# An output projection by seven half-size products, with weight sums made earlier on VectorE

## The chip, the cores and the metric

The kernel runs on one core of a Trainium2 chip. The metric is the time of one execution in device microseconds. Each core has five engines that run their own instruction streams side by side: TensorE (PE, matrix products; its weight loads are listed apart as PEld), VectorE (DVE), ScalarE (ACT), GpSimd (POOL) and SyncE (SP, which issues most transfers). They wait for each other by semaphores. Matrix products are summed in PSUM, which the kernel uses as eight banks of 128 x 512 fp32; all other tiles lie in SBUF, 128 partitions wide.

## The reference

One layer of a decoder with two token mixers, for 1024 tokens and a width of 1024:

```python
h = rmsnorm(x, norm_g)
proj = h @ w_in                                  # split into the parts below
o_gla = gla_chunked(g_q, g_k, g_v, log_a)        # gated linear attention, 4 heads
y_a = (rmsnorm(o_gla, gla_norm_g) * silu(g_gate)) @ w_pa
y_b = (stick_breaking(s_q, s_k, s_v) * silu(s_gate)) @ w_pb     # 8 heads
gates = sigmoid(m_logits + b_gate)
merged = gates[0] * y_a + gates[1] * y_b
out = rmsnorm(x + merged @ w_o, final_g)
```

The change is about the last line: `merged` and `w_o` are both 1024 x 1024. All is fp32 in and out.

## The kernel before, in words

**Products in two halves.** Each fp32 operand of a large product is split into a high part in the matmul's own fp32 format and a low part, the rest: ScalarE writes `hi` (a copy that rounds), VectorE writes `lo = src - hi` (`split`, lines 158 and 159). A product is then three matmuls: hi x hi, hi x lo and lo x hi. Operands that are used as a 1024 x 1024 matrix lie in four quarters (`quarter`): 512 tokens (half n) by the even or the odd blocks of 128 of the inner dimension (parity), each as a pair of tiles of 4 x 512 columns.

**Seven products.** Most parts of `w_in` (28 blocks of 256 columns, `pair_job`) already go by Winograd's form of Strassen's method: with sums of quarters of the activations (S1 to S4, made once) and sums of the quarters of the weight block (`tt`: T1 to T4, four GpSimd instructions per block, lines 233 to 236), seven half-size products (`unit` 0 to 6) replace eight. `Pairs.run(n)` issues the next n of the 28 x 7 units, with the loads and splits of the next blocks between them. A unit is 12 matmuls of 512 columns into one of three PSUM banks (`pp`); VectorE (line 296) or ScalarE (line 265) evicts, and a later unit of the same block adds into the same bank after that.

**The stages.** (1) Norm of x, transposes, the first value columns. (2) The remaining value columns, with S1 to S4. (3) Units of the pairs; over the first 22 of them the GLA decays are computed (`djobs`, pool `dq`), then come 27 units with nothing beside them, `pairs.run(49 - len(djobs))`. (4) The GLA recurrence (from line 683), four units between two steps. Its small factors `fac` (lines 689 to 693) are VectorE instructions, its q, k and v are loaded by SP (lines 701, 702, 711). (5) Stick-breaking attention, filled with `w_pa` products. (6) The `w_pb` products with the merge (`m_half`): 8 column blocks of 128 by 2 token halves, each 24 matmuls; the result is scaled by the gate, the other branch is added, and both halves of the split are written to the four quarters `mq` that stay in SBUF. (7) The output projection.

**The output projection before** (lines 1048 to 1093) works by blocks of 128 tokens: the block's slice of `mq` is the stationary operand, `w_o` the moving one. Columns 0 to 255 come first for all eight token blocks (`proj_n` with `wsA`), while the other 768 columns of `w_o` are loaded and split into `wB`; then for each token block 512 and 256 columns. That is 8 x 24 x 3 = 576 matmuls, 192 of 512 and 384 of 256 columns. `finish` adds x to the bank on VectorE, squares on ScalarE with a running sum, and multiplies by `final_g`; after the last part, `r` is made (VectorE, then a power on GpSimd), VectorE scales columns 0 to 639 and ScalarE the rest, and SP and ACT store them.

**What sets the order.** Instructions are written in program order and a scheduler reorders those of each engine at build time; inside `manual_schedule` the named engines keep the written order. At run time each engine works strictly in its order; a waiting instruction holds all behind it. Buffers of a pool rotate: a tile's next user waits until the last one is done.

Of the kernel before, what the change touches and what calls it, by code (L numbers as in the profile page):

```python
# [9 lines left out]
F32 = mybir.dt.float32  # L10
F32R = mybir.dt.float32r
# [4 lines left out]
P = 128  # L16
# [83 lines left out]
def hybrid_layer(ctx: ExitStack, tc: tile.TileContext, x, norm_g, w_in, w_up, b_dec,  # L100
# [32 lines left out]
    d_a21 = dram_set("a21", 2, [P, 4, HALF])  # L133

# [528 lines left out]
    pairs.run(49 - len(djobs))  # L663
    dq_ctx.close()

# [336 lines left out]
    pq = ctx.enter_context(tc.tile_pool(name="pq", bufs=1, reuse_waits="tile"))  # L1002
    pb_ctx = ExitStack()
# [5 lines left out]
    mq = {}  # L1009
# [22 lines left out]
    mq.update(quads_in(a21b, "m"))  # L1032

    def m_half(pt, eb, n):
        o = stage().bitcast(F32)
        merge_gate(o[:, 0], d_gb, 8, eb, n)
        nc.sync.dma_start(o[:, 1], d_ma[eb][:, half(n)])
        nc.vector.tensor_mul(o[:, 0], pt, o[:, 0])
# [5 lines left out]
    for eb in range(KB):  # L1044
        line += ([pb_load(eb + 2)] if eb + 2 < KB else []) + [pb_unit(eb, 0), pb_unit(eb, 1)]
    Line(line).run()

    wsA = rows_of(load_w256(w_o, 0))
    fg = pq.tile([P, D], F32, tag="fg", name="fg", bufs=1)
    nc.sync.dma_start(fg, final_g.partition_broadcast(P))  # L1050
    xA = pq.tile([P, NT, DV], F32, tag="xA", name="xA", bufs=1)
    nc.sync.dma_start(xA, x2[:, 0:DV].rearrange("(b p) c -> p b c", p=P))
    ssq = pq.tile([P, NT, 3], F32, tag="ssq", name="ssq", bufs=1)
    pb_ctx.close()
    po = ctx.enter_context(tc.tile_pool(name="po", bufs=2, side="right", reuse_waits="tile"))
    wB = [[po.tile([P, D - DV], F32R, tag=f"wo{s}{k}", name=f"wo{s}{k}", bufs=1) for k in range(KB)]
          for s in "hl"]
    ygA = po.tile([P, NT, DV], F32, tag="ygA", name="ygA", bufs=1)
    for kb in range(KB):
        raw = raw_tile().rearrange("p a b -> p (a b)")[:, 0:D - DV]  # L1060
        nc.sync.dma_start(raw, w_o[kb * P:(kb + 1) * P, DV:D])
        split(raw, wB[0][kb], wB[1][kb])
# [54 lines left out]
```

## Time and profile before

| | |
|---|---|
| timed runs, median of 3 | 1256.83 us (1254.66 to 1257.61) |
| the profiled execution | 1258.84 us, its span 1256.8 us |
| PE busy | 1229.9 us, 98% of the span |
| VectorE, ScalarE, GpSimd busy | 768.6, 538.5, 275.0 us |
| mean granted clock of TensorE | 0.995 |
| moved by DMA | 212.08 MB, 169 GB/s |
| output projection | from 1159.89 us, last matmul starts 1250.31 |

Times in rows are microseconds from the span's start. A row of the timeline gives start, duration, engine, line, operation, `out<-in`; in brackets the idle time ahead of it and what ended it. A row of groups gives the same with the count, then busy time and mean ns of one, then idle time ahead. A row of windows gives the window and its length, then busy time and count of PE, PEld, DVE, ACT and POOL, the granted clock, the DMA share and GB/s. A row of DMA issues ends in KB of each and the median us from issue to landing. Matmuls are pipelined: one of 512 columns is shown as 0.39 us long, while the next starts about 0.23 us after it.

### The profile page before, as it was taken

The page shows a single profiled execution, that of the slowest core. Times are in us where ns is not written, and L with a number is a line of the kernel's source. Part 1 is how long each engine was busy: PE and PEld are TensorE (multiplying, and loading weights), DVE is VectorE, ACT ScalarE, POOL GpSimd, SP SyncE. Part 2 cuts the span into 40 slices and gives each one's busy share as a digit, 9 for nine tenths or more (in the row PEclk, how much of TensorE's full clock was granted, in tenths as well). Part 3 has the DMA queues.
Part 4 walks back from the last instruction along what each step waited for, and adds up shares of the span by engine and source line. Part 5 has one row for each costly group of instructions (what it writes and reads, how often), then busy time and mean ns, then how long its engine had stood idle before and what let it go on. Part 6 is the DMA issues. An engine that isn't in the chain of part 4 may idle for free. (4 is left out here: it accounts for less than half of the span.)

```text
span 1256.8 us, 18168 instructions
## 1 busy us (share of the span) xinstructions
PE 1229.9 (98%) x6579; PEld 1034.1 (82%) x6579; DVE 768.6 (61%) x1313; ACT 538.5 (43%) x1042; POOL 275.0 (22%) x296
## 2 busy tenths in 40 slices
PE   8999999999999999999999999999889999999998
PEld 8999878888888888888888878778777878888986
DVE  5474874456655676666654367778867775354533
ACT  5344663344344444444433244445554554233322
POOL 2495331322242242332323010000100000000010
PEclk9999999999999999999999999999989999999999
DMA  7553456555564555755535755444675438553232
GB/s 270 185 172 107 151 190 189 166 155 175 166 199 140 165 187 172 227 172 193 183 124 169 248 160 157 161 155 152 206 222 167 139 105 275 175 167 112 83 117 93
DMA packets 191574, 212.08 MB, mean 169 GB/s; under 512 B 11478, under 2 KB 145644, under 8 KB 188924
## 3 DMA queue, kind: packets, MB, share of 16 engines
q1 hardware_dynamic: 190332, 209.34, 51.4%
q10 hardware_dynamic: 1152, 1.57, 0.3%
q8 instruction: 52, 0.85, 0.3%
q14 instruction: 38, 0.31, 0.1%
HBM read 133.28 MB, written 77.59 MB: 168 GB/s over the span
## 5 line engine op out<-in xcount | busy, mean ns | idle before, releaser
L159 DVE TENSOR_TENSOR wl<-tt,wh 128x1024 fp32r<-128x1024 f32 x56 | 69.0, 1232 | 73.1 <-ACT wh L158 72.8
L296 DVE TENSOR_TENSOR f<-pp,f 128x512 f32<-128x512 f32 x84 | 57.9, 689 | 91.0 <-PE pp L261 87.2
L158 ACT ACTIVATE wh<-raw 128x1024 fp32r<-128x1024 f32 x57 | 60.2, 1058 | 95.9 <-PE pp L260 48.8
L159 DVE TENSOR_TENSOR wl<-raw,wh 128x1024 fp32r<-128x1024 f32 x57 | 80.0, 1405 | 33.3 <-ACT wh L158 32.4
L158 ACT ACTIVATE wh<-tt 128x1024 fp32r<-128x1024 f32 x56 | 59.3, 1059 | 83.0 <-PE pp L260 82.4
L875 POOL TENSOR_SCALAR_AFFINE_SELECT be<-be 128x128 f32<-128x128 f32 x64 | 22.9, 359 | 282.1 <-ACT be L867 214.6
L265 ACT ACTIVATE f<-pp 128x512 f32<-128x512 f32 x84 | 49.6, 591 | 73.0 <-PE pp L261 67.9
L233 POOL TENSOR_TENSOR tt<-raw 128x512 f32<-128x512 f32 x28 | 38.5, 1375 | 184.6 <-DVE wl L159 153.0
L873 DVE TENSOR_TENSOR_SCAN eb<-eb 128x128 f32<-128x128 f32 (+6 forms) x56 | 71.8, 1282 | 5.6 <-ACT eb L866 3.1
L220 POOL TENSOR_TENSOR r<-r,nhalf 128x1 f32<-128x1 f32 x40 | 23.7, 593 | 207.9 <-DVE r L219 207.9
L866 ACT ACTIVATE eb<-z 128x384 f32<-128x384 f32 (+4 forms) x96 | 48.4, 505 | 42.1 <-PE z L864 28.7
L158 ACT ACTIVATE ath<-tr 128x512 fp32r<-128x512 f32 (+2 forms) x96 | 44.0, 496 | 37.9 <-PE tr L892 37.0
L159 DVE TENSOR_TENSOR atl<-tr,ath 128x512 fp32r<-128x512 f32 (+2 forms) x96 | 51.1, 545 | 6.3 <-ACT ath L158 6.3
L909 PE MATMUL av<-atl,v 128*128 128x256 f32 x160 | 47.2, 295 | 3.9 <-DVE atl L159 3.9
L892 PE MATMUL tr<-ident,be 128*128 128x128 f32 x288 | 44.8, 279 | 5.1 <-DVE be L878 4.2
L197 PE MATMUL pp<-bh,wh 128*128 128x512 f32 x128 | 49.8, 389 | 0.0
L198 PE MATMUL pp<-bl,wh 128*128 128x512 f32 x128 | 49.8, 389 | 0.0
L199 PE MATMUL pp<-bh,wl 128*128 128x512 f32 x128 | 49.8, 389 | 0.0
L878 DVE TENSOR_TENSOR be<-be,eb 128x128 f32<-128x128 f32 (+3 forms) x64 | 48.3, 754 | 2.4 <-DVE eb L873 0.5
L892 PEld LDWEIGHTS tr<-ident,be 128*128 128x128 f32 x288 | 32.9, 141 | 19.9 <-DVE be L878 9.9
L867 ACT ACTIVATE be<-z 128x384 f32<-128x384 f32 (+4 forms) x96 | 49.0, 512 | 0.0
L550 ACT ACTIVATE o<-o,vcol 128x512 f32<-128x512 f32 x32 | 23.1, 723 | 59.0 <-DMA o<-d_gb 35.4
(411 smaller groups left out, 4045.8 us busy)
## 6 DMA issues: line engine op xcount, KB each, us to landing
raw<-in_w_in_dram SPq DMA_DIRECT2D x31, 1024.0 KB, 6.0
d_v<-o SPq DMA_DIRECT2D x32, 256.0 KB, 3.0
d_gv<-o SPq DMA_DIRECT2D x32, 256.0 KB, 3.8
v<-d_gv SPq DMA_DIRECT2D x32, 256.0 KB, 3.3
d_q<-o SPq DMA_DIRECT2D x16, 512.0 KB, 4.3
d_k<-o SPq DMA_DIRECT2D x16, 512.0 KB, 5.2
k<-d_k SPq DMA_DIRECT2D x8, 1024.0 KB, 5.1
v<-d_v SPq DMA_DIRECT2D x8, 1024.0 KB, 7.2
```

The lines of the kernel that those rows point to most:

```text
L158: nc.scalar.activation(hi, src, AF.Copy)
L159: eng.tensor_sub(lo, src, hi.bitcast(F32))
L197: nc.tensor.matmul(pt, whi[:, kb], h_, start=kb == 0, stop=False)
L198: nc.tensor.matmul(pt, whi[:, kb], l_, start=False, stop=False)
L199: nc.tensor.matmul(pt, wlo[:, kb], h_, start=False, stop=kb == KB - 1)
L265: nc.scalar.activation(t[nm], t[bank], AF.Copy)
L296: nc.vector.tensor_add(add, bank, add)
L866: nc.scalar.activation(om[:, osl], zt[:, 0:w], AF.Sigmoid, scale=-inv_sqrt)
L867: nc.scalar.activation(be[:, osl], zt[:, 0:w], AF.Sigmoid, scale=inv_sqrt)
L873: nc.vector.tensor_tensor_scan(rest, rest, rest, om[:, T - P:T - P + 1], op0=ALU.mult, op1=ALU.min)
L878: nc.vector.tensor_mul(be[:, off:T], be[:, off:T], om[:, off + 1:T + 1])
L892: nc.tensor.transpose(pt[:, b * P:(b + 1) * P], be[:, c:c + P], ident)
```

## The change

The output projection, too, goes by the seven products, over both token halves and both column halves of `w_o` at once.

- **Sums of w_o.** T1 to T4 of `w_o` (four sums of 128 x 512 for each of four row pairs) are made by VectorE among the 27 units after the decays, and stored to DRAM (`d_t`). SP loads and stores around them. These units now run one at a time with these jobs between them; the pool `dq` is closed ahead of them.
- **Sums of merged.** In stage 6 only the first token half is split at once (A11, A12). GpSimd makes S1 to S4 from the four pieces of each block pair, SP stores S1 to S4 and A22 to DRAM (`d_s`). The last two blocks run in the order (6,0), (7,0), (6,1), (7,1). B11 and B21 of `w_o` are loaded and split between the units, and T1, T2 and most of S2 are loaded.
- **The products.** 28 items of 12 matmuls of 512 columns: seven products by four blocks of 128 tokens, in seven PSUM banks (four `xb`, three `pp`). x is loaded in whole rows. VectorE adds each bank to its x block right after the item (for the first five somewhat later), ScalarE squares when a half row is complete, VectorE applies `r` and `final_g` in one instruction. The other operands are loaded and split item by item (`parts`, `loads`). PE, ACT and DVE keep the written order.

VectorE in the 27 units after the decays, before, from the copies of the decays' last columns (`ebl`) on; `f<-pp,f` is an eviction, `wl`, `dl` and `o` are low halves:

```order
L647 COPY ebl<-e 128x16
L159 TENSOR_TENSOR wl<-tt,wh 128x1024
L689 MEMSET fac 128x48 x2
L690 TENSOR_TENSOR fac<-ebl 128x8
L692 COPY fac<-ebl 128x8
L693 COPY fac<-ebl 128x8
L691 COPY fac<-fac 128x8
L690 TENSOR_TENSOR fac<-ebl 128x8
L692 COPY fac<-ebl 128x8
L693 COPY fac<-ebl 128x8
L296 TENSOR_TENSOR f<-pp,f 128x512
```

The same engine there with the change (`t<-t` is a sum of `w_o`):

```order
L299 TENSOR_TENSOR f<-pp,f 128x512
L162 TENSOR_TENSOR wl<-raw,wh 128x1024
L162 TENSOR_TENSOR o<-tr,o 128x512
L681 TENSOR_TENSOR t<-t 128x512 x3
L162 TENSOR_TENSOR wl<-tt,wh 128x1024
L681 TENSOR_TENSOR t<-t 128x512
L299 TENSOR_TENSOR f<-pp,f 128x512
L681 TENSOR_TENSOR t<-t 128x512 x3
L299 TENSOR_TENSOR f<-pp,f 128x512
```

The `fac` block has gone from here to two weight blocks later (behind the last sums), and three sums in a row stand ahead of evictions.

VectorE in the output projection before, for one token block:

```order
L1067 TENSOR_TENSOR y<-pp,y 128x512
L1070 TENSOR_TENSOR yg<-y,fg 128x512
L1085 TENSOR_SCALAR pre<-ssq 128x1
L1067 TENSOR_TENSOR y<-pp,y 128x256
L1070 TENSOR_TENSOR yg<-y,fg 128x256
L1087 TENSOR_SCALAR r<-ssq,pre 128x1
L1090 TENSOR_SCALAR yg<-yg,r 128x640
```

With the change, from the add of item 14 (a first-half block, product S4 x B22) to that of item 17, the last row, which is the first use of the last x block:

```order
L1209 TENSOR_TENSOR ya<-pp,ya 128x512
L1146 TENSOR_TENSOR mS3l<-raw,mS3h 128x1024
L1225 TENSOR_SCALAR pre<-ssq,pre 128x1
L1209 TENSOR_TENSOR y<-pp,y 128x512
L1234 SCALAR_TENSOR_TENSOR ya<-ya,pre,fg 128x1024
L1146 TENSOR_TENSOR mS3l<-raw,mS3h 128x1024
L1209 TENSOR_TENSOR ya<-pp,ya 128x512
L1146 TENSOR_TENSOR wT4l<-tt,wT4h 128x1024
L1225 TENSOR_SCALAR pre<-ssq,pre 128x1
L1209 TENSOR_TENSOR ya<-pp,ya 128x512
```

Adds now alternate with low halves of operands that later items need. SP's last rows with the change:

```order
L1126 DMA raw<-d_sA_182 128x1024
L1126 DMA raw<-d_sA_183 128x1024
L1230 DMA out_dram<-ya 128x1024
L1184 DMA ya<-in_x_dram 128x1024
L1230 DMA out_dram<-ya 128x1024 x3
L1230 DMA out_dram<-y 128x512 x3
L1230 DMA out_dram<-ya 128x512
```

The one x load among the stores is that last block's (`ya` has four buffers, and it is the fifth tile).

The diff, cut to its core:

```diff
     manual.close()
-    pairs.run(49 - len(djobs))
     dq_ctx.close()
...
+    def t_load(j):
+        wt[j] = tq.tile([P, 4, HALF], F32, tag="t", name="t")
+        for two in range(2):
+            nc.sync.dma_start(wt[j][:, 2 * two:2 * two + 2], ...)
+    def t_sum(j, i):
+        dst, x1, x2_ = ((0, 1, 0), (1, 3, 1), (3, 3, 0), (2, 2, 3))[i]
+        nc.vector.tensor_sub(wt[j][:, dst], wt[j][:, x1], wt[j][:, x2_])
+    def t_store(j):
+        nc.sync.dma_start(d_t[j][:], wt[j])
+    tjobs = [[] for _ in range(49 - len(djobs))]
+    for j in range(4):
+        tjobs[5 * j].append((t_load, (j,)))
+        for i in range(4):
+            tjobs[5 * j + 4 + i].append((t_sum, (j, i)))
+        tjobs[5 * j + 9].append((t_store, (j,)))
+    for jobs in tjobs:
+        pairs.run(1)
+        for fn, args in jobs:
+            fn(*args)
...
     def m_half(pt, eb, n):
...
         nc.vector.tensor_mul(o[:, 0], pt, o[:, 0])
-        nc.vector.tensor_add(o[:, 0], o[:, 0], o[:, 1])
-        q = mq[n, eb % 2]
-        split(o[:, 0], q[0][:, eb // 2], q[1][:, eb // 2])
+        nc.vector.tensor_add(m, o[:, 0], o[:, 1])
+        if n == 0:
+            hi, lo = op[("A11", "A12")[e]]
+            split(m, hi[:, j], lo[:, j])
+    def m_sums(j):
+        return [m_sum(j, "S1", (1, 0), (1, 1), ALU.add), m_sum(j, "S2", "S1", (0, 0), ALU.subtract),
+                m_sum(j, "S4", (0, 1), "S2", ALU.subtract), m_sum(j, "S3", (0, 0), (1, 0), ALU.subtract)]
...
-    for tb in range(NT):
-        finish(tb, 0, 0, proj_n(wsA, mq, tb), xA[:, tb], ygA[:, tb])
-    for tb in range(NT):
...
+    def product(bank, a, b, t, first):
+        (ah, al), w = op[a], op[b]
+        cs = slice(t * P, (t + 1) * P)
+        for j in range(4):
+            bh, bl = ...
+            nc.tensor.matmul(bank, ah[:, j, cs], bh, start=first and j == 0, ...)
+            nc.tensor.matmul(bank, ah[:, j, cs], bl, ...)
+            nc.tensor.matmul(bank, al[:, j, cs], bh, ...)
...
+    def evict_c(u, t):
+        if u == 4:
+            scale(0, t, slice(0, D))
+            put(0, t, nc.sync, slice(0, D))
+        elif u == 5:
+            nc.vector.tensor_mul(ys[1, t][:, half(1)], ys[1, t][:, half(1)], fg[:, half(1)])
+        elif u == 6:
+            scale(1, t, half(0))
+            put(1, t, nc.sync, half(0))
+            nc.scalar.activation(ys[1, t][:, half(1)], ys[1, t][:, half(1)], AF.Copy, scale=pre[1, t][:, 1:2])
+            put(1, t, nc.scalar, half(1))
...
+        product(bank, *(("A11", "B11"), ("A12", "B21"), ("S2", "T2"), ("S1", "T1"), ("S4", "B22"), ("S3", "T3"),
+                        ("A22", "T4"))[u], t, u in (0, 1, 3))
...
+    items = ([(u, t) for u in range(3) for t in range(4)] + [(3, 0), (3, 1), (4, 0), (3, 2), (4, 1), (3, 3), (4, 2), (4, 3)] +
+             [(u, t) for u in (5, 6) for t in range(4)])
+    ev_at = {0: [], 1: [], 2: [], 3: [0, 1], 4: [2, 3, 4]}
...
+    for k, it in enumerate(items):
+        item(*it)
+        mine = [items[e] for e in ev_at.get(k, [k])]
+        for e in mine:
+            evict_a(*e)
+        for e in late:
+            evict_c(*e)
+        for nm, js in parts.get(k, []):
+            o_lo(nm, js)
+        if k in loads:
+            o_load(*loads[k])[0]()
+        his(k + 1)
+        for e in mine:
+            evict_b(*e)
+        late = mine
+        if k == 15:
+            y_load(1, 3)
```

More of the change, by code (lines that the diff above doesn't have):

```diff
@@ L1058, in hybrid_layer @@
[L1058 to L1062, printed above, removed]
-    def finish(tb, k, c0, pt, y, yg):
-        n = y.shape[-1]
-        nc.vector.tensor_add(y, pt, y)
-        junk = ps.tile([P, HALF], F32, tag="tr", name="junk")
-        nc.scalar.activation(junk[:, 0:n], y, AF.Square, accum_out=ssq[:, tb, k:k + 1])
-        nc.vector.tensor_mul(yg, y, fg[:, c0:c0 + n])
@@ L1096 @@
+    manual.close()
 _INS = ["x", "norm_g", "w_in", "w_dec_up", "b_dec", "gla_norm_g", "w_pa", "w_pb", "b_gate",
```

199 lines of the change are left out of this document (167 added, 32 removed).

## The prediction

> **What bounds the kernel now.** I read the page first, then the chain of waits, then the table by stage for the output projection, then single rows.
>
> ```profile
> span 1256.8 us, 18168 instructions
> PE 1229.9 (98%) x6579; PEld 1034.1 (82%) x6579; DVE 768.6 (61%) x1313; ACT 538.5 (43%) x1042; POOL 275.0 (22%) x296
> GB/s 270 185 172 107 151 190 189 166 155 175 166 199 140 165 187 172 227 172 193 183 124 169 248 160 157 161 155 152 206 222 167 139 105 275 175 167 112 83 117 93
> by line: PE pp L198 17.2%; PE pp L199 17.2%; PE pp L197 17.0%; PE pp L210 11.6%; PE pp L211 11.6%; PE pp L212 11.6%; DVE eb L873 2.1%; PE av L909 1.3%; PE av L910 1.2%; PE av L908 1.1%; DVE be L878 1.0%; PE tr L892 1.0%; issue 0.6%; DVE eb
> 1159.89:1250.40 90.51, 90.51 (x577) 81.96 (x575) 39.81 (x79) 23.05 (x60) 7.02 (x15) 1.00 0.31 103
> ```
>
> TensorE is busy for 98% of the span. The fourth row is the chain of waits from 1000 us on: its shares are matmuls, and L210 to L212 (34.8% together) are the output projection. In the last row, the projection's own stretch, the first two numbers after the window say it all: 90.51 us long, 90.51 us of PE busy, at a granted clock of 1.00. VectorE works 39.8 us there, ScalarE 23.1, the DMA share is 0.31 at 103 GB/s. Nothing but matmuls sets this stage's length, so fewer matmuls shorten it, as long as the new operands come in time.
>
> The stage's edges, and the speed of matmuls of 512 columns in two stages (start, duration):
>
> ```profile
> 1124.76 0.39 PE L198 MATMUL pp<-bl,wh 128*128 128x512 f32 x1
> ...
> 1137.45 0.39 PE L197 MATMUL pp<-bh,wh 128*128 128x512 f32 x1
> 1159.89 0.28 PE L210 MATMUL pp<-wh,ma11h 128*128 128x256 f32 x1
> 1191.38 0.40 PE L210 MATMUL pp<-woh,ma11h 128*128 128x512 f32 x1
> ...
> 1195.80 0.40 PE L211 MATMUL pp<-wol,ma11h 128*128 128x512 f32 x1
> 1250.31 0.28 PE L212 MATMUL pp<-woh,ma22l 128*128 128x256 f32 x1
> ```
>
> In the stage ahead (the first pair) 57 starts lie in the listing, 56 steps in 12.69 us: 0.2266 us each. In the projection (the second pair) 20 starts, 19 steps in 4.42 us: 0.2326. The last matmul starts at 1250.31 and takes a slot of 0.12, so the projection fills 1159.89 to 1250.43: 90.54 us.
>
> **The change part by part.** *Products.* All 576 matmuls of the projection go: -90.54. In come 7 products x 4 blocks of 128 tokens = 28 items of 12 matmuls, 336 of 512 columns. Their moving operand lies in tiles of 4 x 512 columns, as in the stage at 0.2266; their stationary operand is a 128-column slice of activations, as in the projection at 0.2326. Neither row is nearer, so I take the middle: 336 x 0.2296 = 77.2 us, between 76.1 and 78.2.
>
> [...]
>
> *Work beside the products.* Groups of the last 200 us (busy, mean ns):
>
> ```profile
> L159 DVE TENSOR_TENSOR wl<-raw,wh 128x1024 fp32r<-128x1024 f32 x10 | 12.2, 1219 | 5.0 <-ACT wh L158 5.0
> L1067 DVE TENSOR_TENSOR y<-pp,y 128x512 f32<-128x512 f32 x8 | 5.5, 691 | 26.4 <-PE pp L212 23.3 <-DMA out_dram<-yg 3.1
> L1087 DVE TENSOR_SCALAR r<-ssq,pre 128x1 f32<-128x1 f32 x8 | 1.7, 214 | 1.0 <-ACT junk L1069 0.2
> L158 ACT ACTIVATE wh<-raw 128x1024 fp32r<-128x1024 f32 x10 | 10.5, 1055 | 9.2 <-PE pp L198 8.6 <-DMA raw<-in_w_pb_dram 0.6
> L379 DVE SCALAR_TENSOR_TENSOR xs<-xt,r,gb x8: 1273/1276/1289, 6.4 to 37.9; 128x1024 f32<-128x1024 f32 x8
> L550 ACT ACTIVATE o<-o,vcol 128x512 f32<-128x512 f32 x20 | 14.4, 720 | 51.2 <-DMA o<-d_gb 35.4 <-issue 8.0 <-DMA o<-d_ga 6.6
> ```
>
> VectorE in the new stage: 28 adds x 0.69 = 19.3; low halves of ten operands, 20 x 1.22 = 24.4; four scalings of 1024 columns x 1.28 = 5.1; eight of 512 x 0.69 = 5.5; 16 small x 0.21 = 3.4: together 57.7 of 77 us. ScalarE: 20 high halves x 1.06, 16 squares x 0.79, 4 copies x 0.72: 36.7. Both fit under the products, each operand's halves are made some five items ahead of its first matmul, and cost nothing while nobody falls behind. If VectorE does fall behind, see the second rival. The multiplications of the stage ahead (L197 to L199) stay as they are in number; eight splits of 512 columns leave it, four of 1024 and sixteen sums on the idle GpSimd enter: nothing on the path, bounds 0 to +2.
>
> *The one wait that I can place.* The fifth x block of the second token half takes the first block's buffer: SP stores block 0, then loads over it, and VectorE's add of item 17 waits for that load with everything behind it. Item 19 adds into the same bank and may not start before that add.
>
> ```profile
> out_dram<-yg SPq DMA_DIRECT2D x8, 320.0 KB, 3.0
> y<-in_x_dram SPq DMA_DIRECT2D x8, 384.0 KB, 3.0
> raw<-in_w_pb_dram SPq DMA_DIRECT2D x8, 512.0 KB, 4.7
> d_e<-e SPq DMA_DIRECT2D x4, 512.0 KB, 2.6
> ```
>
> With an item of 12 x 0.2296 = 2.755 us: item 15 ends 44.3 us into the stage, its add 45.0, the scaling of block 0 46.3, the store of 512 KB lands 3.0 later (49.4 with its issue), the load 3.5 later (53.0; both taken from the rows' 2.6 to 4.7), the add ends at 53.7. Item 19 is due at 19 x 2.755 = 52.3. So PE waits 1.4 us; with 2.6 for each transfer it is 0, with 4.7 it is 4.3.
>
> *The end.* What follows the last matmul, and the same steps at 512 columns:
>
> ```profile
> 1239.34 0.69 DVE L1067 TENSOR_TENSOR y<-pp,y 128x512 f32<-128x512 f32 x1 [3.07 <-PE pp L212]
> 1240.06 0.60 ACT L1069 ACTIVATE junk<-y 128x512 f32<-128x512 f32 x1 [3.74 <-DVE y L1067]
> 1240.60 0.19 ACT L1069 ACTIVATION_READ_ACCUMULATOR junk<-y 128x1 f32 x1
> 1250.63 0.42 DVE L1067 TENSOR_TENSOR y<-pp,y 128x256 f32<-128x256 f32 x1 [1.15 <-PE pp L212]
> 1251.09 0.39 ACT L1069 ACTIVATE junk<-y 128x256 f32<-128x256 f32 x1 [1.86 <-DVE y L1067]
> 1251.41 0.19 ACT L1069 ACTIVATION_READ_ACCUMULATOR junk<-y 128x1 f32 x1
> 1252.57 0.61 ACT L1092 ACTIVATE yg<-yg,r 128x384 f32<-128x384 f32 x1 [0.97 <-POOL r L1088]
> 1253.21 0.34 ACTq L1093 DMA_DIRECT2D out_dram<-yg  x1
> ```
>
> From 1250.43 to 1256.8 it takes 6.37 us. The last piece is now 512 columns wide: add to square 0.72 instead of 0.46, square to read-out 0.54 instead of 0.32, last scaling about 0.72 instead of 0.61: +0.6. Block 26's 512 KB are also sent only then, some 1.5 us ahead of the last block's; before, the last 512 KB had the queues to themselves. I add 0.4 of a possible 1.2: +1.0, between 0.6 and 1.8.
>
> *The sums of w_o.* 16 subtractions of 128x512 on VectorE, 8 loads and 4 stores of 1 MB on SP, between the end of the decays and the recurrence.
>
> ```profile
> 170.00:250.00 80.00, 78.44 (x351) 64.01 (x350) 44.20 (x59) 31.20 (x42) 23.73 (x22) 1.00 0.59 194
> 180.20 1.29 POOL L233 TENSOR_TENSOR tt<-raw 128x512 f32<-128x512 f32 x1 [15.07 <-DVE fac L689]
> 180.22 1.30 DVE L690 TENSOR_TENSOR fac<-ebl 128x8 f32<-128x8 f32 x1
> 184.82 0.66 PE L564 MATMUL tr<-ident,f 128*128 128x128 f32 x4 [1.02 <-DVE f L296]
> 214.52 0.50 PE L259 MATMUL pp<-ha22h,wh 128*128 128x512 f32 x1 [0.35 <-DVE f L296]
> ```
>
> VectorE has 35.8 us free in these 80 us, and 16 x 0.69 = 11 go in. PE lost 1.56 us there: 1.02 because a block of `fac` instructions stood ahead of an eviction, 0.35 behind a split that waited for ScalarE. By the order the first group now stands some 50 us later and the second some 20, the sums in their place. An eviction has one product of 2.7 us to be done in, less its own 0.69; three sums in a row take 2.07, which just fits. I take 0, between -1.4 (the two waits gone, none new) and +5 (below).
>
> The 128x8 subtraction that took 1.30 us ended with the GpSimd sum that began with it. [...]
>
> Priced by the rows: 16 x (0.69 + 1.29) = 31.7 us at most, still under 35.8; but three such sums ahead of an eviction take 5.9 instead of 2.0, and PE would wait up to some 4 us once, or 1.3 at each of the four blocks. The first heads' v, q and k are loaded behind the new loads and stores on SP, some 20 us later than now, and their first matmul is at 261.0 us:
>
> ```profile
> L723 PE MATMUL pa<-q,ke x64: 272/298/324, 261.0 to 654.5; 128*64 128x128 f32 x64
> 208.68 0.32 SPq L701 DMA_DIRECT2D qe<-d_gq  x1
> ```
>
> The q load, at 208.68 now, has 50 us to lose; I cost it at nothing.
>
> *Sum.* -90.54 + 77.2 + 1.4 + 1.0 + 0 = -10.9. It is made against a profiled execution of 1258.84 us, whose span of 1256.8 leaves 2.04 around it; the timed median is 1256.83, 2.0 below that execution, and I take the same difference from it: 1256.83 - 10.9 = 1245.9 us. The best ends give -90.54 + 76.1 + 0 + 0.6 - 1.4 = -15.2 (1241.6), the worst -90.54 + 78.2 + 4.3 + 1.8 + 5 + 2 = +0.8; these are five independent terms and won't all be worst, so the likeliest case itself spans 1242.5 to 1249.
>
> **Rivals.** *Transfers become the bound (slower).* The new stage moves x and out (8.4 MB), three quarters of S1 and a quarter of S2, six whole operands of 1.05 MB and three late stores of 0.26: 16.5 MB, where the old one moved 9.3 (90.51 us x 103 GB/s). At the 169 GB/s that the page gives as the mean, that takes 97.6 us: -90.54 + 97.6 + 1.0 = +8.1, 1265 us. It decides once the rate falls under 16.5 / 89.5 = 184 GB/s. Against it: one slice of 31 us reached 275 GB/s, and every load is issued two items or more ahead. Chance 5%.
>
> *VectorE's written order becomes the bound.* For items 12 to 19 a bank is added to twice in turn, and each add has one item to be done in. VectorE is 75% full there and takes its work strictly in order, so one late operand or x block delays all that follows. If items 14 to 19 each wait 1 us, 6 - 1.4 = 4.6 are added: 1250.5. For it speaks the wait that I placed; against it 17 free us. 12%.
>
> *The w_o sums stall the pairs.* If each block of four sums meets GpSimd's sums as the 128x8 row did, PE waits 1.3 us at each of the four: +5, 1251. For it speak the two short waits there now, against it VectorE's 35.8 free us and sums that mostly fall between GpSimd's. 8%. [...]
>
> That the change doesn't do what it says I exclude: PE's order has the 336 products and lacks the 576.
>
> **How the numbers follow.** Forecast 75%, the rivals 5, 12 and 8%. Timed runs lie 3 us apart, so less than 0.2% (2.5 us) can't be told from no change. Faster than 1254.3: nearly all of the forecast and most of the second and third rival, 0.91; within: their far ends, 0.04; slower: the first rival and mishaps that I don't see, 0.05. The range takes in the forecast's own and the middle of two rivals: 1242.5 to 1251.
>
> **What would show it.** In the changed profile the first item starts near 1160, as L210 does now; PE is busy without a break for some 77 us but for one gap near 52 us into it, ahead of item 19, that ends with VectorE's add, which waited for x. Steps of 0.227 or 0.233 settle the first term. About 7.4 us lie between the last matmul and the end. Between 180 and 255 us the unit starts are within 1.5 us of now. I am wrong if PE shows gaps at each operand's first item (transfers or splits), if the stage starts later than 1162, or if the pairs have slipped by more than 2 us.

## The result and the profile after

The changed kernel takes 1246.47 us (median, 1245.47 to 1247.65) against 1257.22 us for the kernel before: a ratio of 0.9919, with a 95% interval of 0.9901 to 0.9936. The forecast was 1245.9. The profiled execution took 1247.65 us, its span is 1245.8 us, so it is compared with the span of 1256.8 before: 11.0 us gained, 10.9 forecast. The sum came out right, but two of its terms did not.

The new output projection in the table by stage, first its whole length, then up to the gap:

```profile
1161.35:1238.57 77.22, 76.45 (x337) 62.80 (x335) 55.96 (x76) 28.34 (x50) 12.20 (x11) 1.00 0.54 192
1161.35:1213.00 51.65, 51.65 (x229) 42.60 (x227) 37.12 (x45) 19.65 (x29) 9.46 (x6) 1.00 0.69 244
```

TensorE's timeline at its start, at the gap and at its end:

```profile
1161.35 0.39 PE L1200 MATMUL xb<-wB11h,mA11h 128*128 128x512 f32 x1
...
1212.80 0.39 PE L1202 MATMUL pp<-wB22h,mS4l 128*128 128x512 f32 x1
1213.95 0.50 PE L1200 MATMUL pp<-wB22h,mS4h 128*128 128x512 f32 x1 [0.77 <-DVE ya L1209]
1214.29 0.39 PE L1201 MATMUL pp<-wB22l,mS4h 128*128 128x512 f32 x1
...
1238.34 0.39 PE L1202 MATMUL xb<-wT4h,mA22l 128*128 128x512 f32 x1
```

The stage is 77.22 us long. In the first 51.65 us TensorE has no gap: 227 steps of 0.2267 us lie between 1161.35 and 1212.80. Then comes the one gap, ahead of item 19, whose first matmul (1213.95) starts 1.15 us after the one before it instead of 0.23, and the next step is 0.34: 1.04 us lost. The rest is 336 x 0.2267 = 76.2. VectorE is busy 56.0 us of the 77, and the transfers run at 244 GB/s up to the gap; TensorE waits for them nowhere else.

The gap's chain in VectorE's timeline (the scaling of block 0 and the add of item 17), then in SP's (the store of block 0 and the load over it), then the load's row among the DMA issues from 1206 us on:

```profile
1205.67 1.27 DVE L1234 SCALAR_TENSOR_TENSOR ya<-ya,pre,fg 128x1024 f32<-128x1024 f32 x1
...
1213.21 0.69 DVE L1209 TENSOR_TENSOR ya<-pp,ya 128x512 f32<-128x512 f32 x1 [3.26 <-PE pp L1202]
```

```profile
1206.98 0.34 SPq L1230 DMA_DIRECT2D out_dram<-ya  x1
1209.61 0.33 SPq L1184 DMA_DIRECT2D ya<-in_x_dram  x1
```

```profile
ya<-in_x_dram SPq DMA_DIRECT2D x1, 512.0 KB, 3.5
```

Block 0 is scaled by 1206.94, its store is issued at 1206.98, SP can load over it from 1209.61, and VectorE, idle for 3.26 us, adds at 1213.21. The row names PE as the releaser, but item 17 had ended at 1210.3; the add waited for the load, 3.5 us after its issue. It is the chain that was foreseen, some 0.7 us earlier at its start.

The end of the kernel, from the timeline of all engines:

```profile
1238.77 0.69 DVE L1209 TENSOR_TENSOR ya<-xb,ya 128x512 f32<-128x512 f32 x1 [1.02 <-PE xb L1202]
...
1241.99 0.35 ACTq L1230 DMA_DIRECT2D out_dram<-ya  x1
```

The last matmul's slot ends at 1238.34 + 0.23 = 1238.57, the span at 1245.8: 7.23 us, where 6.37 + 1.0 = 7.37 were forecast.

That the projection starts at 1161.35 and not at 1159.89 was not foreseen. The time is lost among the pairs, as the table by stage shows there:

```profile
200.00:230.00 30.00, 27.71 (x115) 22.37 (x114) 20.22 (x23) 7.15 (x9) 9.77 (x7) 0.94 0.92 308
215.00:221.00 6.00, 5.80 (x18) 4.62 (x19) 5.17 (x9) 1.06 (x1) 0.00 (x0) 0.72 0.72 264
```

The two loads of the third group of `w_o` rows in SP's timeline, with the store that SP issues between them, and the sums and the eviction in VectorE's:

```profile
202.55 0.96 SPq L676 DMA_DIRECT2D t<-in_w_o_dram  x1
206.30 0.33 SPq L525 DMA_DIRECT2D d_gq<-f  x1
206.69 0.42 SPq L676 DMA_DIRECT2D t<-in_w_o_dram  x1
```

```profile
208.59 0.69 DVE L681 TENSOR_TENSOR t<-t 128x512 f32<-128x512 f32 x1 [1.19 <-DMA t<-in_w_o_dram]
212.12 0.69 DVE L681 TENSOR_TENSOR t<-t 128x512 f32<-128x512 f32 x1 [2.83 <-DMA t<-in_w_o_dram]
...
214.47 0.68 DVE L299 TENSOR_TENSOR f<-pp,f 128x512 f32<-128x512 f32 x1
```

TensorE's timeline there, and the row of the recurrence's first product:

```profile
212.53 0.39 PE L264 MATMUL pp<-S4h,dl 128*128 128x512 f32 x1
215.20 0.50 PE L262 MATMUL pp<-ha22h,wh 128*128 128x512 f32 x1 [2.29 <-DVE f L299]
...
216.76 0.63 PE L262 MATMUL pp<-ha22h,wh 128*128 128x512 f32 x1
217.19 0.63 PE L263 MATMUL pp<-ha22l,wh 128*128 128x512 f32 x1
```

```profile
L755 PE MATMUL pa<-q,ke x64: 272/298/324, 263.3 to 656.8; 128*64 128x128 f32 x64
```

The two loads are issued at 202.55 and 206.69, in a stretch with a DMA share of 0.92 at 308 GB/s, and the sums can start on them 6.0 and 5.4 us later. That is what loads of `w_o` take here (5.0 to 6.8 us from issue to landing): the second is late because it is issued late. SP works in order and stood 2.7 us at the store in the second row, whose data VectorE had not written yet, since VectorE was itself waiting for a load (2.81 us, until 205.58). Two sums that wait 1.19 and 2.83 us for the loads, a low half and a third sum stand ahead of an eviction in VectorE's order; the eviction runs at 214.47, and TensorE waits for it. From 212.53 to 215.20 are 2.67 us, 2.45 more than a step. And the wait costs more than itself: from 216.76 on seven steps of 0.427 us follow each other and one of 0.36, with a granted clock of 0.72 from 215 to 221 us, another 1.6 us. Up to 185 us the changed kernel is 1.25 us *ahead* of the kernel before; from 220 us on it is 2.32 behind, and the recurrence's first product starts at 263.3 instead of 261.0. In the attention stage that lead or lag shifts again in each execution (below); in this one 1.46 us of it are left at the projection.

The sum by its terms, each against the span of 1256.8:

| term | forecast | profiled execution |
|---|---|---|
| the old 576 matmuls | -90.54 | -90.54 |
| 336 products | +77.2 (76.1 to 78.2) | +76.2 |
| the wait ahead of item 19 | +1.4 (0 to 4.3) | +1.04 |
| the end | +1.0 (0.6 to 1.8) | +0.86 |
| sums of `w_o` among the pairs | 0 (-1.4 to +5) | +2.32 at the recurrence, +1.46 at the projection |
| all | -10.9 | -11.0 |

### The profile page after: what moved, and what is told of

Its sections match the earlier page's. It is cut to its first block, busy times and chain, and to the rows that moved or that the text cites. A ratio compares the mean times of both kernels' runs of the same rounds, so it can differ in the third digit from the quotient of the medians.

```text
span 1245.8 us, 17778 instructions
## 1 busy us (share of the span) xinstructions
PE 1214.7 (98%) x6339; PEld 1013.8 (81%) x6339; DVE 801.1 (64%) x1321; ACT 544.9 (44%) x1030; POOL 303.6 (24%) x304
## 3 DMA queue, kind: packets, MB, share of 16 engines
q10 hardware_dynamic: 576, 1.05, 0.2%
```

## The experiments

### The late loads of w_o

Theory A: the wait at 215 us comes from sums that stand ahead of evictions and wait for loads that are issued too late. Theories B and C put it on VectorE's sums beside GpSimd's, and on the mass of bytes. The first run moves the loads:

```diff
-    tq = ... tc.tile_pool(name="tq", bufs=2, ...)
+    tq = ... tc.tile_pool(name="tq", bufs=3, ...)
-        tjobs[5 * j].append((t_load, (j,)))
+        tjobs[max(5 * j - 3, 0)].append((t_load, (j,)))
```

> The changed kernel with the loads of w_o for the sums issued three units earlier (units 0, 2, 7, 12 instead of 0, 5, 10, 15), into three buffers instead of two; nothing else is changed. In the changed kernel TensorE loses 2.45 us ahead of 215.2 us, and its next eight matmuls run at 0.427 us instead of 0.227; from there on everything is 2.32 us later than before the change, after having been 1.25 us ahead. Theory A (late load): VectorE's first sums of the third block stand 1.19 and 2.83 us for transfers issued at 202.55 and 206.69, and an eviction waits behind them. By it the wait and the slow matmuls go, the recurrence starts 1.3 us earlier than before the change instead of 2.3 later (3.6 us gained there), and the time falls by 2 to 3.6 us, to 1243 to 1244.5. Theory B (VectorE's sums beside GpSimd's, my third rival): the time of a sum does not depend on when its load was issued, so a wait of about 2 us stays in this stage and the time stays at 1246.5 +- 0.7. Theory C (too many bytes, the DMA share is 0.92 to 1.05 from 200 to 210 us): the earlier loads make another transfer late, of the weight blocks or the decay factors, and at most 1.5 us are gained.

1244.3 us (1242.98 to 1245.76), ratio to the kernel before 0.9894 (0.9879 to 0.9909). The wait in TensorE's timeline, and the recurrence's first product:

```profile
214.18 0.50 PE L262 MATMUL pp<-ha22h,wh 128*128 128x512 f32 x1 [0.68 <-DVE f L299]
```

```profile
L755 PE MATMUL pa<-q,ke x64: 272/298/324, 260.7 to 654.2; 128*64 128x128 f32 x64
```

The wait shrinks from 2.29 to 0.68 us, the slow matmuls are gone, and the recurrence starts 0.3 us earlier than before the change: 2.6 of the 3.6 us expected. It is theory A, since a sum lasts as long as it did; the first sum of the third block still waits 0.52 us for its load.

The second run leaves the 16 subtractions out and keeps the transfers:

```diff
-        for i in range(4):
-            tjobs[5 * j + 4 + i].append((t_sum, (j, i)))
```

> The changed kernel without the 16 subtractions; the loads and stores of w_o stay where they are, so what is loaded as T1 to T4 is plain w_o and the output is not the reference's. Theory A (VectorE waits for late loads): the wait at 215 us goes, as with earlier loads: 3.6 us gained at the recurrence, 1243 to 1244.5 in all, within 0.6 of the run with earlier loads. [...] Theory C (bytes): the wait stays in some other instruction's name, within 1 us of 1246.5.

1242.15 us (1241.19 to 1243.0), ratio 0.9876 (0.9863 to 0.989). The table by stage, and the recurrence's first product:

```profile
200.00:230.00 30.00, 30.00 (x134) 24.82 (x133) 13.67 (x17) 8.83 (x12) 9.21 (x7) 1.00 0.88 301
```

```profile
L753 PE MATMUL pa<-q,ke x64: 272/298/324, 259.3 to 652.8; 128*64 128x128 f32 x64
```

With the same transfers (301 GB/s) and nothing that waits for them on VectorE, TensorE has no gap in these 30 us. So the bytes alone cost nothing here: theory C falls. The recurrence starts 1.7 us earlier than before the change. That fits the two short waits which the prediction's bounds held to be gone with the moved block of `fac` instructions (-1.4). This run is 2.15 us below the one with early loads, not within 0.6, though the ranges of their times touch; 1.4 us of that stand in the recurrence's start. With early loads TensorE still waited 0.84 us more than a step; how much of the rest VectorE's time for the sums takes (0.68 to 1.67 us each there) is not shown.

The third puts the sums alone into the kernel before:

```diff
-    pairs.run(49 - len(djobs))
     dq_ctx.close()
+    ... t_load, t_sum, t_store, tjobs as in the change ...
+    for jobs in tjobs:
+        pairs.run(1)
+        for fn, args in jobs:
+            fn(*args)
```

> The kernel before, with the loads, sums and stores of w_o among the 27 units exactly as in the change, and nothing that uses them. Theory (the sums are the only part of the change that costs time ahead of the output projection): TensorE's wait of about 2.4 us near 215 us and eight matmuls at 0.427 us appear here too, the recurrence starts 2.0 to 2.7 us later than before, and the time rises by 1 to 3 us, to 1258 to 1260. Rival (the cost comes from something else in the change, the place of other tiles or of the small factors): the recurrence starts within 0.7 us of before and the time within 0.7 of 1257.2.

1258.02 us against 1257.01, ratio 1.0011 (1.0 to 1.0023): about 1 us slower. The wait and the recurrence:

```profile
215.18 0.79 PE L260 MATMUL pp<-ha22h,wh 128*128 128x512 f32 x1 [2.13 <-DVE f L297]
```

```profile
L752 PE MATMUL pa<-q,ke x64: 272/298/324, 263.2 to 656.8; 128*64 128x128 f32 x64
```

The wait is there (2.13), eight slow steps stand behind it, and the recurrence starts 2.2 us later than before. So all that the change costs ahead of the projection comes from the sums of `w_o`. The time at the end is only 1 us longer; the rest is inside the differences from one execution to the next.

### The wait ahead of item 19

```diff
+    yh = py.tile([P, HALF], F32, tag="yh", name="yh", bufs=1)
+    nc.sync.dma_start(yh, x2[D - P:D, half(1)])
     ...
-            y_load(1, 3)
+            ys[1, 3] = po.tile([P, D], F32, tag="ya", name="ya", bufs=4)
+            nc.sync.dma_start(ys[1, 3][:, half(0)], x2[D - P:D, half(0)])
```

> The changed kernel with a tile of its own for the second column half of the last x block, loaded with the other x blocks at the start of the output projection; only its first half, which the very last item needs, still goes into the first block's buffer. Theory (the reload is the whole reason for the gap ahead of item 19, which costs 0.93 us and then 0.11 in the next matmul): the gap is gone, nothing takes its place, and the time falls by 1.0 us, to 1245.4. Rival (VectorE's written order is the bound there, my second rival): VectorE is 75% busy and the gap comes back as one or more shorter waits at items 14 to 19, so that less than 0.4 us is gained.

1245.06 us (1243.76 to 1249.03), ratio 0.9905 (0.9888 to 0.9922). The stage from its first matmul to the end of the last one's slot:

```profile
1164.00:1240.17 76.17, 76.17 (x337) 62.88 (x335) 56.07 (x76) 28.36 (x50) 12.21 (x11) 1.00 0.54 195
```

The projection is 76.17 us long instead of 77.22, and TensorE is busy for all of it: 1.05 us gained, as forecast, with nothing in its place. So the reload was the whole wait, and VectorE's written order (the second rival) costs nothing once no x block is late. The time agrees (1.4 us lower), but its interval is too wide to show 1 us by itself.

### Both together

> Both edits together: earlier loads of w_o into three buffers, and a tile of its own for half of the last x block. If the two costs are independent, the gains add: 3 to 4.6 us below the changed kernel, 1242 to 1243.5, which would be the fastest version. If the attention stage, which is not bound by TensorE all the time, takes back what is gained ahead of it (in the changed kernel 2.32 us of delay became 1.46 behind it), only 2 to 3 us are gained.

1244.28 us (1241.87 to 1246.16), ratio 0.9892 (0.9875 to 0.9908).

```profile
L755 PE MATMUL pa<-q,ke x64: 272/298/324, 259.9 to 653.4; 128*64 128x128 f32 x64
```

```profile
1159.26:1235.42 76.16, 76.16 (x337) 62.90 (x335) 56.07 (x76) 28.36 (x50) 12.21 (x11) 1.00 0.53 195
```

In the profile both gains are there: the recurrence starts 1.1 us before that of the first kernel, and the stage is 76.16 us long. The time is 2.2 us below the changed kernel and level with early loads alone: the case in which only 2 to 3 us are gained. Why it isn't lower shows between the two stages: at the recurrence this execution is 1.1 us ahead of the first kernel's, at the projection 0.63. With early loads alone it was 0.3 ahead at the recurrence and 2.96 at the projection. The attention stage in between moves by some 2 us from one execution to the next (the last section).

### Is a long wait dearer than itself?

In the kernel with a tile of its own for half of the last x block, needless work on VectorE makes two waits of known place:

```diff
+        for _ in range({12: 7, 17: 9}.get(k, 0)):
+            nc.vector.tensor_tensor(fg[:, half(0)], fg[:, half(0)], fg[:, half(0)], op=ALU.max)
         for e in mine:
             evict_a(*e)
```

> The kernel with a tile of its own for half of the last x block (no gap ahead of item 19), with needless work put on VectorE: seven maxima of 128x512 of final_g with itself ahead of the add of item 12, and nine ahead of that of item 17, 0.6 us from start to start. TensorE must then wait 1.4 us ahead of item 14 and 3.1 ahead of item 19. Theory A (a wait of over some 2 us costs more than itself, because the matmuls behind it run at half speed for a while): behind the first gap no matmul takes more than 0.35 us and it costs 1.4 to 1.6 us; behind the second some eight matmuls take 0.427 instead of 0.227 and it costs 3.1 + 1.6 = 4.7 us. Theory B (the slow matmuls in the stage of the pairs came from the dense transfers there, not from the gap): both gaps cost only themselves.

One execution, 1253.88 us. TensorE's timeline (the steps of the second group are the differences of the first numbers):

```profile
1200.26 0.47 PE L1205 MATMUL pp<-wB22h,mS4h 128*128 128x512 f32 x1 [2.13 <-DVE y L1214]
...
1217.96 0.79 PE L1205 MATMUL pp<-wB22h,mS4h 128*128 128x512 f32 x1 [3.83 <-DVE yh L1214]
1218.56 0.63 PE L1206 MATMUL pp<-wB22l,mS4h 128*128 128x512 f32 x1
1218.98 0.63 PE L1207 MATMUL pp<-wB22h,mS4l 128*128 128x512 f32 x1
```

The needless maxima took 0.72 instead of 0.6 us each, so the waits are longer than meant: 2.29 and 3.99 us beyond a step. Behind the first no matmul is slow. Behind the second, twelve steps are slow, ten of them 0.427: 2.5 us more. In the 5 us of that wait nothing is transferred, by the table by stage:

```profile
1213.00:1218.00 5.00, 1.18 (x7) 0.64 (x5) 4.83 (x8) 0.00 (x0) 0.00 (x0) 0.83 0.00 0
```

So dense transfers are not the reason, and theory B falls. Theory A holds for the second wait, but the first, over 2 us too, cost only itself. More waits can be read from the other profiled executions, since the wait near 212.5 us comes back in each version that has the sums as the change has them:

| wait beyond a step, us | where | steps of 0.34 to 0.60 us behind it |
|---|---|---|
| 0.84, 1.42 | pairs, early loads; pairs, sums on GpSimd | 0, 0 |
| 1.81, 2.05 | pairs | 0, 0 |
| 2.01, 2.12 | pairs | 8, 8 |
| 2.29 | projection (above); pairs, sums alone | 0; 8 |
| 2.45, 2.48 | pairs (the changed kernel; own x tile) | 8, 7 |
| 3.99 | projection (above) | 12 |

Up to 1.8 us a wait cost only itself, from 2.0 to 2.3 it cost some 1.6 us more in three cases and nothing more in two, and from 2.45 on it cost 1.6 to 2.5 us more. Its length alone does not decide; what does is in the last section.

### Are transfers near the bound in the projection?

```diff
+        if 1 <= k <= 9:
+            nc.sync.dma_start(d_x[k - 1][:], d_s[("S4", "S3", "A22")[k % 3]][1][:])
```

> The same kernel without that work, with nine needless copies of 512 KB from DRAM to DRAM issued by SP in the output projection's first ten items, among the loads that the items need: 4.7 MB read and 4.7 MB written beside some 12.6 MB in 52 us. Theory (transfers are far from the bound): no operand comes late, TensorE waits less than 1 us in the stage. Rival (my first rival: transfers are near the bound): the loads behind the copies come late, TensorE waits at the first items of T3, S3, T4 or A22, 5 us or more in all.

One execution, 1245.67 us. Up to the place of the former gap:

```profile
1160.00:1211.00 51.00, 51.00 (x227) 42.23 (x226) 38.72 (x47) 20.10 (x29) 9.46 (x6) 1.00 0.87 335
```

At 335 GB/s and a DMA share of 0.87 TensorE is busy for all 51 us, and the whole stage stays at 76.16. The first rival, with its limit of 184 GB/s, was far off: the mean rate of the page was no bound.

### The sums on GpSimd

```diff
-        nc.vector.tensor_sub(wt[j][:, dst], wt[j][:, x1], wt[j][:, x2_])
+        nc.gpsimd.tensor_tensor(wt[j][:, dst], wt[j][:, x1], wt[j][:, x2_], op=ALU.subtract)
```

> The version with earlier loads and a tile of its own for half of the last x block, with the 16 sums of w_o on GpSimd instead of VectorE. Theory (what costs time is that sums which wait for their loads stand ahead of evictions on VectorE): with nothing of theirs on VectorE the recurrence starts 1.7 us earlier than in the kernel before, as in the run without sums, against 1.1 earlier with the sums on VectorE and early loads; the time falls by another 0.3 to 0.8 us, to 1242 to 1244. [...]

1241.77 us (1241.44 to 1242.25) against 1257.62, ratio 0.9877 (0.9861 to 0.9894): the lowest time of a version that computes all, though its interval overlaps with that of the sums on VectorE with early loads. The reason expected for it is not what the profile shows. GpSimd's timeline, ScalarE's, TensorE's, and the recurrence:

```profile
187.00 19.14 POOL L681 TENSOR_TENSOR t<-t 128x512 f32<-128x512 f32 x12 [0.62 <-PE pp L264]
206.10 1.29 POOL L236 TENSOR_TENSOR tt<-raw 128x512 f32<-128x512 f32 x1
```

```profile
209.91 1.06 ACT L161 ACTIVATE wh<-tt 128x1024 fp32r<-128x1024 f32 x1 [4.47 <-POOL tt L237]
```

```profile
211.51 0.50 PE L262 MATMUL pp<-S4h,dh 128*128 128x512 f32 x1 [1.26 <-ACT f L268]
```

```profile
L755 PE MATMUL pa<-q,ke x64: 272/298/324, 260.7 to 654.2; 128*64 128x128 f32 x64
```

Twelve sums stand in one row on GpSimd ahead of the next weight block's own sums, which start at 206.1 us instead of 198.4. ScalarE waits 4.47 us for those with an eviction behind it, TensorE waits 1.26 us for that eviction, and the recurrence starts 0.3 us earlier than before the change, not 1.7. So half of the theory holds: VectorE no longer waits for these loads, but the next block's sums are late. Of the low time, 2.8 us were gained in the attention stage of this profiled execution, where the version does nothing else than the others.

### What sets the step of 0.2326 us before the change

The prediction took the middle of two steps, 0.2266 and 0.2326. The changed kernel has the first throughout. Four runs looked for the cause of the second. Two change the tiles of the moving operand in the kernel before:

```diff
-    wB = [[po.tile([P, D - DV], ...) for k in range(KB)] for s in "hl"]
+    wB = [[[po.tile([P, n], ...) for n in (HALF, DV)] for k in range(KB)] for s in "hl"]      # first run
+    wB = [[po.tile([P, KB, n], ...) for n in (HALF, DV)] for s in "hl"]                       # second run
```

> The kernel before, with the 768 columns of w_o that are the moving operand kept in separate tiles of 512 and 256 columns instead of tiles of 768; the matmuls, their order and their stationary operands are the same. Theory A (the layout of the moving tile sets the step): the 512-column matmuls of the output projection go from steps of 0.228 to 0.241, 0.2326 on average, to even steps of 0.227, as in the changed kernel, and the projection gets about 192 x 0.006 = 1.1 us shorter. Theory B (the stationary operand, the four quarters of merged, or the change between 512 and 256 columns sets it): the steps stay at 0.232 to 0.233.

> The kernel before, with the moving operand of w_o in one tile of 8 x 512 columns and one of 8 x 256 for each half of the split, so that the 512-column rows lie 2048 bytes apart; in the run with separate tiles of 512 and 256 columns the rows may have kept their old distance of 3072 bytes, since the tiles were made in turn. Theory A (the distance or place of the moving rows): the 512-column steps of the output projection become an even 0.227. Theory B (something else): they stay uneven at 0.232 on average.

1257.02 and 1258.04 us, one execution each. The first item of 24 matmuls in the timeline of the first run:

```profile
1189.70 0.40 PE L210 MATMUL pp<-woh,ma11h 128*128 128x512 f32 x1
...
1195.05 0.39 PE L212 MATMUL pp<-woh,ma12l 128*128 128x512 f32 x1
```

There are 23 steps in 5.35 us, 0.2326 each. The same item of the second run starts its first and its last matmul at 1190.62 and 1195.97, 5.35 us apart too, and in both runs the stage takes as long as before. Theory A is out. The other two put matmuls of 256 columns between those of 512, in the version with a tile of its own for half of the last x block:

```diff
+            for c in ([slice(0, DV), slice(DV, HALF)] if mix[0] else [slice(0, HALF)]):
+                nc.tensor.matmul(bank[:, c], ah[:, j, cs], bh[:, c], ...)      # and the two others
     ...
+        mix[0] = (u, t) in ((1, 1), (2, 1))      # first run
+        mix[0] = (u, t) == (0, 1)                # second run
+            if a == "A11":                       # second run
+                ah, al = op[("A11", "A12")[j % 2]]
```

> The version with a tile of its own for half of the last x block, in which two of the 28 items (the sixth and the tenth) do each of their matmuls as two of 256 columns: 24 instead of 12 matmuls for the same result. Theory A (matmuls of 256 columns in between are what set the 0.2326 us of the kernel before): in the items behind each of the two the 512-column steps become uneven, 0.228 to 0.241 and 0.232 on average. Theory B (the stationary operand, which in the kernel before changes between two quarters every three matmuls, sets it): all 512-column steps stay at 0.2267, and only the two items themselves take longer, 24 x 0.120 = 2.88 us instead of 2.72.

> The version with a tile of its own for half of the last x block, in which the four items of the first product take their stationary slices in turn from A11 and A12, changing after every three matmuls as the kernel before does, and the second of them in matmuls of 256 columns; the result is then not the reference's, and only the steps are read. Theory A (the change of the stationary quarter keeps the steps uneven once matmuls of 256 columns have made them so): the first item's steps are 0.227 or 0.232, and the 24 behind the 256-column ones stay uneven at 0.232 on average. Theory B (it plays no part): after some five uneven steps behind the 256-column matmuls all are 0.2267 again.

In the first of these two the result is, against what was written, not the reference's. The edit starts the sum in each half of a bank on its own in the first of the two items; whether that is why, no run shows. The number and the sizes of the matmuls are as said, and only they are read here. It took 1245.89 us. Behind its first halved item:

```profile
1174.11 0.28 PE L1208 MATMUL pp<-wB21h,mA12h 128*128 128x256 f32 x1
...
1176.99 0.40 PE L1208 MATMUL pp<-wB21h,mA12h 128*128 128x512 f32 x1
...
1178.15 0.39 PE L1210 MATMUL pp<-wB21h,mA12l 128*128 128x512 f32 x1
1178.37 0.39 PE L1208 MATMUL pp<-wB21h,mA12h 128*128 128x512 f32 x1
```

The 24 matmuls of 256 columns take 2.88 us. The five steps behind them are uneven (0.233, 0.236, 0.228, 0.233, 0.231), then all are 0.2267 again. With the stationary operand changing between two quarters (1248.68 us) it is the same: five uneven steps, then even ones. So neither the place of the moving rows nor 256 columns in between nor the change of quarters keeps the steps at 0.2326. What does stays open.

## Why the prediction was right, and where it was not

**What bounds the kernel.** Right: TensorE was busy without a gap in the old stage, and fewer matmuls made it 13.3 us shorter (90.54 to 77.22).

**The products, 77.2.** The mechanism was right, the size 1.0 too high. The step that failed is "neither row is nearer, so I take the middle": the stage ran at the row of the stage ahead, 0.2267, which makes 76.2 us without waits.

**The one wait that I can place, 1.4.** Right in place, chain and kind, 0.4 too long: the load took the 3.5 us that were put in, but SP could issue it 2.7 us after the scaling instead of 3.1. That all of it began some 0.7 us earlier is no reason, since shorter items bring the matmuls that wait forward as well. Taking the wait away gave back 1.05 us.

**The end, +1.0.** Measured 0.86.

**The sums of w_o, 0.** Wrong, though inside its bounds: 2.32 us later at the recurrence than before the change, and 4.0 us later than in the run without the sums (263.3 against 259.3). Of the terms this was costed with most care for VectorE (its free time, GpSimd's sums beside its own) and with none for when the sums' own loads land. The step that failed is "an eviction has one product of 2.7 us to be done in ... three sums in a row take 2.07, which just fits": it takes the sums' operands to be there (and 2.07 is even a little more than 2.7 less 0.69). They were not: the loads landed 5.0 to 6.8 us after their issue, and the one that mattered was issued 4.1 us after the one before it. Part of this could be read from the profile of before: the window from 170 to 250 us had a DMA share of 0.59 at 194 GB/s, and 4 MB loaded and 4 MB stored in some 50 us add an estimated 160 GB/s. After the change the same window has a share of 0.87. The prediction weighed transfers in the projection, where they held up no matmul but at the one reload, and not here. But dense transfers alone cost nothing, as the run without sums shows (301 GB/s and no gap from 200 to 230 us); it took an instruction that waits for them ahead of evictions. The prediction also priced any wait at its own length, while this one cost 1.6 us more.

**The rivals.** The third named the right place for another reason, and not the right shape: it had a wait of 1.3 us at each of the four weight blocks, +5 in all, and there was one wait of 2.45 us, for a load. Its reason is seen too, but holds up no matmul:

```profile
221.80 5.02 DVE L681 TENSOR_TENSOR t<-t 128x512 f32<-128x512 f32 x3 [0.30 <-DMA t<-in_w_o_dram]
```

The last three sums take some 1.67 us each instead of 0.69 while GpSimd makes its own four (221.58 to 227.97 us, 1.29 to 1.75 us each); the prediction had priced such a sum at 0.69 + 1.29. What lengthens them is not shown. The first rival falls with 335 GB/s, the second with 76.17 us of uninterrupted work.

**What would have shown it.** The start before 1162, the gap 52 us into the stage, steps of 0.227 and 7.4 us at the end all came. That the unit starts between 180 and 255 us would be "within 1.5 us of now" did not come, and the last sign of being wrong, "if the pairs have slipped by more than 2 us", did (2.32): these two told of the miss. That the total came out within 0.1 us is luck: +1.46 at the projection's start was made up for by -1.0 in the products, -0.4 in the wait and -0.1 at the end, and the 1.46 itself are what the attention stage, which moves from one execution to the next, left of 2.32.

**A row of another stage.** The row L379 among the groups of the last 200 us is from 6.4 to 37.9 us. The scaling that it priced at 1.28 us took 1.27.

## What to carry to other kernels

Work that goes into the free time of an engine must be priced with its operands: a sum of 0.69 us that waits 2.8 us for its load is a 2.8 us wait for all that stands behind it on that engine, and whether a load will be late is read from two things, how long loads take to land in that stretch (here 5.0 to 6.8 us) and what stands ahead of it in the issuing engine's order (here a store that held SP for 2.7 us). The DMA share alone does not tell: at 0.87 and 0.88 two runs here lost nothing. In the pairs and the projection a wait of TensorE cost only its length up to 1.8 us; behind six of the eight longer ones, of 2.0 to 4.0 us, seven to twelve steps were slow, most of them 0.427 us instead of 0.227. That breaking one long wait into short ones would be a gain by itself is my estimate from these waits; no run tried it. And a sum that comes out right is not yet a prediction that was right: compare each term with its row, and a start of a stage with its start before.

## What the runs showed of the hardware that I had not expected

**The clock after a wait.** The slow matmuls start 0.427 us apart, and the granted clock over them is 0.50. In the traces such stretches between the first matmuls and the last are 3.41 us long or twice that, and in one execution they start whole multiples of 3.413 us apart: in the kernel before at 886.06 and 927.02 us, twelve times 3.413. In the changed kernel they start at 216.61 and 889.03 us, 197 times 3.4133 apart. On this grid like waits can be told apart. Two waits of 2.0 us beyond a step, the first from the run with two halved items (2.01), the second from the run with needless copies (2.05), by windows of this length:

```profile
212.66:216.07 3.41, 1.56 (x7) 1.00 (x6) 3.41 (x6) 0.63 (x1) 0.00 (x0) 1.00 0.90 296
216.07:219.48 3.41, 3.41 (x10) 2.63 (x9) 2.50 (x5) 0.42 (x1) 0.00 (x0) 0.50 0.85 272
```

```profile
210.72:214.13 3.41, 2.21 (x10) 1.50 (x8) 2.40 (x4) 0.63 (x1) 0.00 (x0) 1.00 0.99 403
214.13:217.55 3.42, 2.74 (x12) 2.28 (x13) 3.42 (x7) 0.00 (x0) 0.00 (x0) 1.00 0.78 259
```

In the first run one window holds the whole wait: TensorE is idle for 3.41 - 1.56 = 1.85 us of it, and the next window is at half clock. In the second the wait lies across two windows, which are idle for 1.20 and 0.68 us, and the clock stays at 1.00. The wait of 2.29 us in the run with needless maxima lies across two windows as well (1.11 and 1.01 us). In the 14 traces, from 60 us to the last matmul, each window at full clock with 1.75 us or more without a matmul was followed by one at half clock, and none with up to 1.67; in between both occur. In the kernel before the windows that were followed so had 2.56 and 1.75 us without a matmul, in the changed kernel 2.40 and 2.01. So about half of such a window without a matmul sufficed in these runs.

**Where the spread between executions comes from.** The attention stage has a wait of 2.3 to 3.4 us beyond a step near 883 us in every profiled execution; behind it the granted clock fell to half in eleven of the 14 and stayed at full in three. The stage's rows in the kernel before, and in the one with the sums on GpSimd:

```profile
850.00:1000.00 150.00, 140.24 (x763) 114.68 (x763) 116.89 (x178) 79.38 (x172) 10.29 (x29) 0.97 0.57 180
```

```profile
850.00:1000.00 150.00, 139.81 (x788) 114.45 (x789) 117.20 (x179) 79.28 (x171) 10.29 (x29) 1.00 0.57 181
```

The granted clock there is 0.97 and 1.00, and in the same 150 us 763 and 788 matmuls are started. Between 860 us and the projection the profiled executions differ by -2.8 to +1.2 us from that of the kernel before, without any change to the stage. That is most of the spread of the timed runs (1254.4 to 1260.1 us for the kernel before), and more than each of the two gains that the experiments were after. The clock has a part in it: the eight executions with a mean granted clock of 0.98 or 1.00 from 870 to 960 us lie between -2.8 and 0.0, the six with 0.94 or 0.96 between -0.6 and +1.2. The ranges overlap, so it need not be all, and no run set the place of the windows on purpose: that the spread comes from it is argued, not shown.
